# Two-layer hybrid decoder on one core: the last two expert pairs of each expert layer summed in one PSUM bank, in chunks of 512, 256 and 256 columns

## The chip, the cores and the metric

One Trainium2 chip, one of its cores. The time is device microseconds (us) from the start to the end of one execution; three executions of the kernel before gave a median of 892.34 us. Engines: PE is TensorE (matmuls; PEld its weight loads), DVE is VectorE, ACT is ScalarE, POOL is GpSimd, SP is SyncE, which here only starts transfers (DMAs). SBUF is the on-chip memory that the engines read, PSUM the banks that PE writes.

## The reference, cut to what matters

The kernel computes two decoder layers on 256 tokens of 1024 channels: an mLSTM mixer, then an attention mixer, and after each a grouped mixture of experts (16 experts, 2 per token, one shared router) and a layer norm. Only the end of the expert part is touched:

```python
def expert_block(args):
    xb, e = args
    return (jax.nn.silu(xb @ w_gate[e]) * (xb @ w_up[e])) @ w_down[e]

ys = lax.map(expert_block, (xs, block_expert)).reshape(cap, D)
y = jnp.zeros((T, D), h.dtype).at[buf_tok].add(ys * buf_w[:, None].astype(ys.dtype))
...
x = layer_norm(DEEPNORM_ALPHA * x + gate[:, None, :] * y, ln_g[layer, 1], ln_b[layer, 1])
```

So each token's output is the sum over its experts of (weight times expert output), times a gate row, added to alpha times the residual, and then normed over the 1024 channels.

## The kernel before, in words

**Tiling.** Tokens lie in two tiles of 128 partitions (`t` = 0, 1); `xt` holds 2 x 1024 channels. Experts go in pairs `b` = 0 to 7, 64 slots for each expert of a pair, so a pair fills 128 partitions. For each pair PE computes `pg` (gate) and `pu` (up), DVE multiplies them to `a`, PE transposes `a` to `aT`, and `down` computes `py` = `aT` times the down weights, a chunk of columns at a time, in bank `bankA`. `outputs` scales a chunk by the slot weights `wsl`, and `combine` multiplies it by the one-hot matrix `ohT[b]`, which brings slots back to tokens: `po`, one bank (`bankB`) for each token tile. Then DVE adds `po` to `acc`, which is `xt`.

**Two forms of the sum.** For pairs 0 to 6 `outputs` splits the scaled chunk into an upper part `yh` (rounded by ACT) and the rest `yl` (by DVE), and PE multiplies both by `ohT` in a fast format and sums them in the bank; `add_gated` (lines 544 to 548) then takes two DVE operations: `lntmpe` = `po` times gate, and `xt` += `lntmpe`. For the last pair (7) the gate is multiplied in before: `yg` = `py` times slot weight times gate (line 1239), a plain fp32 product with `ohT` (two passes on PE), and one DVE addition (line 1226). Pairs 0 to 6 have two chunks of 512 columns, pair 7 four of 256 (`LAST`, line 55).

**Layer norm.** `ln_stats` (line 550) takes `bn_stats` over four pieces of 256 columns for each token tile, `bn_aggr`, a square root on ACT and a reciprocal on DVE. In layer 0 `normalise` (line 566) then scales a whole token tile of 1024 columns, and the next stage transposes `xt` (`tk`, line 511) for the attention's keys. In layer 1 two DVE operations per half tile (lines 1388, 1389) and a store end the kernel.

**What sets the order.** `T` is PE's handle with `T.pinned`: while it is true, PE's instructions stay in program order. In `moe` that is so for nearly all of PE's work. The other engines are ordered by a scheduler by priority, except where `issue_after` puts an instruction behind another. `split` casts a weight tile to its upper part on ACT and takes the rest on DVE, with the priority `AHEAD` = 100. `T.pinned` and the like name no engine code lines of their own: every instruction that goes through a pinned handle is shown at line 135.

**Transfers.** All weights come through SP's one queue in pieces of 512 KB (`pieces`, line 224), each into a slot of a ring of buffers that the piece before has to have left. `ws[b, 2, i]` are the down weights of chunk `i`: a chunk of 512 columns is four pieces (two halves of the rows for each of two experts), a chunk of 256 columns two pieces (one for each expert, all rows).

**The overflow branch.** `rest` is a conditional block that is not taken here; each engine loads a register and branches (lines 1343, 1344). In layer 1 it stands between pair 7's `pu` and the last `down_part`.

## Time and profile before

| what | value |
|---|---|
| median of 3 executions | 892.34 us (891.92 to 893.64) |
| the profiled execution | 893.36 us |
| its span, first to last instruction | 891.7 us |
| PE busy | 854.3 us, 96% |
| DVE busy | 528.1 us, 59% |
| ACT busy | 327.4 us, 37% |
| read from HBM | 316.53 MB, 356 GB/s over the span |
| mean granted TensorE clock | 0.983 |

The span is 1.7 us shorter than the profiled execution's own time, and that execution is 1.0 us over the median. PE is shown busy nearly all the time, but matmuls are pipelined and a PE that works through products while the next weights are on their way looks the same as one that sets the pace; so the stages have to be looked at one by one. The end of layer 0's expert part lies at about 492 to 527 us of the span, that of layer 1 at about 856 us to the end.

### The profile page before, as it was taken

What the parts mean: (1) busy time and instruction counts of PE and PEld (TensorE: products, weight loads), DVE (VectorE), ACT (ScalarE), POOL (GpSimd) and SP (SyncE); (2) the same over time, 40 slices, a digit from 0 to 9 for tenths busy, and PEclk for the clock granted to TensorE, in tenths of its full rate; (3) what the DMA queues carried; (4) which work ended last, traced back from release to release, by engine and by line L of the source; (5) the groups of instructions that cost most, each with busy time, mean ns of one, the idle gap of its engine ahead of it and who ended that gap; (6) DMA issues with size and microseconds to landing.
All of it is one profiled execution on the core that took longest, in us unless ns stands there. A gap on an engine that the chain in (4) does not pass through costs nothing.

```text
span 891.7 us, 13434 instructions
## 1 busy us (share of the span) xinstructions
PE 854.3 (96%) x5049; PEld 532.2 (60%) x5052; DVE 528.1 (59%) x964; ACT 327.4 (37%) x549; POOL 7.8 (1%) x21
## 2 busy tenths in 40 slices
PE   8999999999999799999999889999989999999994
PEld 4888997688787434343343379887763433434332
DVE  2469997688898613342322489999973423233317
ACT  3458666366555411011121046667551111211120
POOL 0020000000000000000000000000000000000000
PEclk9999999999999999999999989999979999999997
DMA  9999887699987899999999999977978999999993
GB/s 324 394 393 351 294 337 251 228 410 413 370 268 258 327 397 407 406 406 407 407 406 407 367 410 412 363 278 258 373 289 310 408 406 407 407 407 407 406 400 120
DMA packets 161921, 318.56 MB, mean 357 GB/s; under 512 B 10120, under 2 KB 28168, under 8 KB 161848
## 3 DMA queue, kind: packets, MB, share of 16 engines
q1 hardware_dynamic: 161704, 317.42, 94.4%
q8 instruction: 42, 0.69, 0.3%
q14 instruction: 31, 0.25, 0.1%
q10 hardware_dynamic: 144, 0.20, 0.1%
HBM read 316.53 MB, written 1.05 MB: 356 GB/s over the span
## 4 chain that ended last, share of the span: by engine, by line
PE 43%; DMA 7%; DVE 3%; ACT 2%; issue 1%; DVEq 0%; SPq 0%; ACTq 0%
PE py L135 9%; PE pg L135 8%; PE pu L135 8%; DMA w<-in_moe_w_up_dram 3%; PE po L135 3%; PE ga L135 3%; DMA w<-in_moe_w_down_dram 2%; DMA w<-in_moe_w_gate_dram 1%; PE bo L1482 1%; PE bk L274 1%; PE bk L275 1%; PE bk L276 1%; PE by L274 1%; PE by L276 1%; PE by L275 1%; PE bq L274 1%
## 5 line engine op out<-in xcount | busy, mean ns | idle before, releaser
L1243 DVE SCALAR_TENSOR_TENSOR yl<-py,wsl,yh 128x512 fp32r<-128x512 f32 x28 | 21.0, 750 | 171.2 <-ACT yh L1242 171.2
L135 PE MATMUL py<-w,aT 128*64 128x512 f32 (+1 forms) x576 | 117.9, 547 | 1.7 <-DMA w<-in_moe_w_down_dram 1.7
L135 PE MATMUL pu<-w,xe 128*64 128x512 f32 x512 | 118.7, 596 | 0.2 <-DMA w<-in_moe_w_up_dram 0.2
L135 PE MATMUL pg<-w,xe 128*64 128x512 f32 x512 | 116.1, 596 | 0.0
L362 DVE SCALAR_TENSOR_TENSOR adacc<-ada,pk,adacc 128x1024 f32<-128x1024 f32 x70 | 89.4, 1278 | 0.2
L135 PEld LDWEIGHTS py<-w,aT 128*64 128x64 f32 x576 | 41.7, 137 | 73.6 <-issue 59.3
L135 PEld LDWEIGHTS pu<-w,xe 128*64 128x64 f32 x512 | 36.0, 137 | 67.5 <-issue 61.3
L135 PEld LDWEIGHTS pg<-w,xe 128*64 128x64 f32 x512 | 34.8, 137 | 63.9 <-issue 58.9
L547 DVE TENSOR_TENSOR lntmpe<-po,gate 128x512 f32<-128x512 f32 x56 | 36.1, 684 | 41.4 <-PE po L135 41.4
L1209 ACT COPY aT<-aT 128x512 f32<-128x512 f32 x16 | 9.4, 585 | 139.4 <-PE aT L135 139.4
L1242 ACT ACTIVATE yh<-py,wsl 128x512 fp32r<-128x512 f32 x28 | 19.2, 687 | 84.3 <-PE py L135 84.3
L525 ACT ACTIVATE xe<-ga,coef 128x256 f32<-128x256 f32 x32 | 16.1, 561 | 72.3 <-PE ga L135 72.3
L274 PE MATMUL z<-hh,wz 128*128 128x256 f32 x128 | 36.4, 284 | 0.0
L548 DVE TENSOR_TENSOR xt<-xt,lntmpe 128x512 f32<-128x512 f32 x56 | 36.0, 682 | 0.0
L275 PE MATMUL z<-hl,wz 128*128 128x256 f32 x128 | 36.0, 281 | 0.0
L276 PE MATMUL z<-hh,wz 128*128 128x256 f32 x128 | 36.0, 281 | 0.0
L1202 DVE TENSOR_TENSOR a<-a,pu 128x512 f32<-128x512 f32 x16 | 11.0, 688 | 36.3 <-PE pu L135 20.3
L135 PE MATMUL ga<-onehot,xh 128*128 128x256 f32 x128 | 31.3, 321 | 0.0
L135 PE MATMUL xm<-hh,win 128*128 128x256 f32 x144 | 28.8, 289 | 0.7 <-ACT hh L135 0.7
L1197 ACT ACTIVATE a<-pg 128x512 f32<-128x512 f32 x16 | 9.6, 597 | 52.2 <-PE pg L135 52.2
L135 PEld LDWEIGHTS ga<-onehot,xh 128*128 128x128 f32 x128 | 24.8, 218 | 5.9 <-DVE xt L548 4.1
L135 PE MATMUL ga<-onehot,xl 128*128 128x256 f32 x128 | 27.6, 282 | 0.0
(386 smaller groups left out, 1886.5 us busy)
## 6 DMA issues: line engine op xcount, KB each, us to landing
w<-in_moe_w_gate_dram SPq DMA_DIRECT2D x128, 512.0 KB, 10.2
w<-in_moe_w_up_dram SPq DMA_DIRECT2D x128, 512.0 KB, 10.2
w<-in_moe_w_down_dram SPq DMA_DIRECT2D x128, 512.0 KB, 10.2
ada<-in_w_ada_dram SPq DMA_DIRECT2D x112, 512.0 KB, 9.2
win<-in_a_w_in_dram SPq DMA_DIRECT2D x16, 512.0 KB, 8.2
wz<-in_a_w_in_dram SPq DMA_DIRECT2D x16, 512.0 KB, 10.0
wout<-in_a_w_out_dram SPq DMA_DIRECT2D x16, 512.0 KB, 8.4
wv<-in_a_wv_dram SPq DMA_DIRECT2D x8, 512.0 KB, 5.4
```

Source lines behind the costliest of these rows:

```text
L135: return self.tc.keep_in_program_order(f(*a, **kw))
L274: T.matmul(ps, l[0], r[0], start=start, stop=False, skip_group_check=True)
L275: T.matmul(ps, l[0], r[1], start=False, stop=False, skip_group_check=True)
L276: T.matmul(ps, l[1], r[0], start=False, stop=stop, skip_group_check=True)
L362: V.scalar_tensor_tensor(acc, w, c, acc, op0=OP.mult, op1=OP.add)
L525: A.activation(dst, ps, AF.Identity, bias=sh[:, k:k + 1], scale=sc[:, k:k + 1])
L547: V.tensor_tensor(tmp, y, gate[:, c], op=OP.mult)
L548: V.tensor_tensor(dst[:, t, c], dst[:, t, c], tmp, op=OP.add)
L1197: A.activation(a, pg, AF.Silu)
L1202: V.tensor_tensor(a, a, pu, op=OP.mult)
L1242: A.activation(yh, py, AF.Copy, scale=wsl[:, b:b + 1])
L1243: V.scalar_tensor_tensor(yl, py, wsl[:, b:b + 1], yh.bitcast(F32), op0=OP.mult, op1=OP.subtract)
```

## The change

- `LAST` gives the last pair three chunks, of 512, 256 and 256 columns. Its output is split into an upper and a lower part like that of the other pairs, in a tile `yl` that takes the place of `yg`.
- `down_last` replaces the last call of `down_part`. It computes pair 6's two chunks and pair 7's first two chunks of `py` before any sum; pair 7's transposes come behind pair 6's first chunk. `add(h)` then sums, for both token tiles, pair 6's two parts and pair 7's two parts of chunk `h` in one bank, so that DVE adds both pairs with one `add_gated`.
- Behind each addition DVE takes the `bn_stats` of the columns just added; `bn_aggr` and the root follow with the last chunk.
- `V.pinned` is set for this part: DVE's instructions keep program order too.
- In layer 0 the norm goes by halves of 512 columns, both token tiles of the first half first. `k_part(0)`, the first work of the attention, is put behind the last norm operation on DVE and now also behind the last root on ACT, and the first three `split` calls take the priorities 100, 35 and 60 from `ahead`.
- In layer 1 the norm's operations are in program order, tile by tile.

```diff
--- before.py
+++ after.py
@@ -52,7 +52,7 @@
 FILL = 8, 4, 14
 LEAD = 1, 4
 PE_ORDER = 1, 0, 4, 3, 2
-LAST = (0, 256), (256, 256), (512, 256), (768, 256)
+LAST = (0, 512), (512, 256), (768, 256)
 PAST = 4
 AT = 2, 6
 BACC = dict(dynamic_dma_scratch_size=1024)
@@ -257,11 +257,13 @@
         return lambda k: v[k // 4][:, k % 4:k % 4 + 2, :]
 
 
+    ahead = deque()
+
     def split(pool, src, name, dst=None, low=None):
 
         if dst is None:
             dst = pool.tile([P, 2, 2, 512], F32R, tag="whl", name=name)
-        with tc.high_priority(AHEAD):
+        with tc.high_priority(ahead.popleft() if ahead else AHEAD):
             A.copy(dst[:, 0], src)
             (low or V).tensor_tensor(dst[:, 1], src, dst[:, 0].bitcast(F32), op=OP.subtract)
         return [(dst[:, 0, i, :], dst[:, 1, i, :]) for i in range(2)]
@@ -1221,29 +1223,22 @@
                 for t in range(NT):
                     po = bankB(f"po{layer}_{b}_{t}{h}")[:, 0:w]
                     oh = ohT[b][:, P * t:P * t + P]
-                    if b == last_b:
-                        T.matmul(po, oh.bitcast(F32), y, start=True, stop=True)
-                        V.tensor_tensor(acc[:, t, o:o + w], acc[:, t, o:o + w], po, op=OP.add)
-                    else:
-                        for i in range(2):
-                            T.matmul(po, oh, y[i], start=i == 0, stop=i == 1)
-                        add_gated(t, o, w, po, gate, f"e{layer}_{b}_", acc)
+                    for i in range(2):
+                        T.matmul(po, oh, y[i], start=i == 0, stop=i == 1)
+                    add_gated(t, o, w, po, gate, f"e{layer}_{b}_", acc)
 
             def outputs(b, h, py):
 
                 o, w = chunks(b)[h]
                 if b == last_b:
-                    if not yg:
-                        yg.append(pm.tile([P, D], F32, tag="xe", name=f"yg{layer}"))
-                    y = yg[0][:, o:o + w]
-                    V.scalar_tensor_tensor(y, py, wsl[:, b:b + 1], gate[:, o:o + w], op0=OP.mult, op1=OP.mult)
-                    return y
-                yh, yl = [pm.tile([P, w], F32R, tag=f"{n}{h % 2}", name=f"{n}{layer}_{b}_{h}") for n in ("yh", "yl")]
+                    yh, yl = [ylast[0][:, z, o:o + w] for z in range(2)]
+                else:
+                    yh, yl = [pm.tile([P, w], F32R, tag=f"{n}{h % 2}", name=f"{n}{layer}_{b}_{h}") for n in ("yh", "yl")]
                 A.activation(yh, py, AF.Copy, scale=wsl[:, b:b + 1])
                 V.scalar_tensor_tensor(yl, py, wsl[:, b:b + 1], yh.bitcast(F32), op0=OP.mult, op1=OP.subtract)
                 return yh, yl
 
-            yg = []
+            ylast = []
 
             held = []
 
@@ -1252,17 +1247,48 @@
                     combine(*h)
                 held.clear()
 
-            def down_part(*pairs, hold=False):
-
-                for b, aT in pairs:
-                    for h, (o, w) in enumerate(chunks(b)):
-                        py = bankA(f"py{layer}_{b}_{h}")[:, 0:w]
-                        down(b, h, py, aT)
-                        if not hold:
-                            combine_held()
-                        held.append((b, h, outputs(b, h, py)))
-                if not hold:
-                    combine_held()
+            def down_chunk(b, h, aT):
+                py = bankA(f"py{layer}_{b}_{h}")[:, 0:chunks(b)[h][1]]
+                down(b, h, py, aT)
+                return outputs(b, h, py)
+
+            def down_part(b, aT):
+
+                for h in range(len(chunks(b))):
+                    held.append((b, h, down_chunk(b, h, aT)))
+
+            def down_last(aT, a):
+
+                y = [down_chunk(last_b - 1, 0, aT)]
+                aT7 = transposed_a(last_b, a, "oh")
+                y.append(down_chunk(last_b - 1, 1, aT))
+                ylast.append(pm.tile([P, 2, D], F32R, tag="xe", name=f"yl{layer}"))
+
+                def add(h):
+                    o, w = chunks(last_b)[h]
+                    po = [bankB(f"po{layer}_{t}_{h}")[:, 0:w] for t in range(NT)]
+                    for z, (oh, vs) in enumerate(((ohT[last_b - 1], [v[:, o % 512:o % 512 + w] for v in y[o // 512]]), (ohT[last_b], y7[h]))):
+                        for t in range(NT):
+                            for i, v in enumerate(vs):
+                                T.matmul(po[t], oh[:, P * t:P * t + P], v, start=(z, i) == (0, 0), stop=(z, i) == (1, 1))
+                    for t, (st, mv, rs) in enumerate(sts):
+                        add_gated(t, o, w, po[t], gate, f"e{layer}_{last_b}_", acc)
+                        for i in range(o // 256, (o + w) // 256):
+                            V.bn_stats(st[:, i, :], xt[:, t, 256 * i:256 * i + 256])
+                        if o + w == D:
+                            V.bn_aggr(mv, st)
+                            roots.append(A.activation(rs, mv[:, 1:2], AF.Sqrt, bias=epsc))
+
+                y7, roots = [], []
+                sts = [[small.tile([P, n], F32, tag=tag, name=f"{tag}n{t}") for tag, n in (("lnst", 24), ("lnmv", 2), ("lnrs", 1))] for t in range(NT)]
+                for s in sts:
+                    s[0] = s[0].rearrange("p (i j) -> p i j", j=6)
+                for h in range(len(chunks(last_b))):
+                    y7.append(down_chunk(last_b, h, aT7))
+                    if h:
+                        add(h - 1)
+                add(h)
+                return [s[1:] for s in sts], roots[-1]
 
             def overflow():
 
@@ -1362,7 +1388,7 @@
                 pg = gate_up(b + 1, xe, 0, "pg", lambda: aT.append(transposed_a(b, a)))
                 a = gated(b + 1, pg)
                 if b + 1 < last_b:
-                    down_part((b, aT[0]), hold=True)
+                    down_part(b, aT[0])
                     if b == AT[layer]:
                         load(b, 2, PAST)
                         T.pinned = False
@@ -1378,19 +1404,25 @@
                 rest()
             T.pinned = True
             preload(AF.Sqrt)
-            down_part((b, aT[0]), (last_b, transposed_a(last_b, a, "oh")))
+            V.pinned = True
+            sts, root = down_last(aT[0], a)
             T.pinned = False
-            for t in range(NT):
-                st = ln_stats(acc, t, f"n{layer}")
-                if last:
-                    for h in range(2):
-                        c = slice(512 * h, 512 * h + 512)
-                        V.scalar_tensor_tensor(acc[:, t, c], acc[:, t, c], st[0], row[0][:, c], op0=OP.subtract, op1=OP.mult)
-                        V.scalar_tensor_tensor(acc[:, t, c], acc[:, t, c], st[1], row[1][:, c], op0=OP.mult, op1=OP.add)
-                        nc.sync.dma_start(out[P * t:P * t + P, c], acc[:, t, c])
-                else:
-                    end = normalise(acc, t, st)
-        return None if last else end
+            if not last:
+                for h in range(2):
+                    c = slice(512 * h, 512 * h + 512)
+                    for t, (mv, rs) in enumerate(sts):
+                        if h == 0:
+                            V.reciprocal(rs, rs)
+                        end = V.tensor_scalar(xt[:, t, c], xt[:, t, c], mv[:, 0:1], rs, op0=OP.subtract, op1=OP.mult)
+                V.pinned = False
+                return end, root
+            for t, (mv, rs) in enumerate(sts):
+                V.reciprocal(rs, rs)
+                for h in range(2):
+                    c = slice(512 * h, 512 * h + 512)
+                    V.scalar_tensor_tensor(acc[:, t, c], acc[:, t, c], mv[:, 0:1], row[0][:, c], op0=OP.subtract, op1=OP.mult)
+                    V.scalar_tensor_tensor(acc[:, t, c], acc[:, t, c], rs, row[1][:, c], op0=OP.mult, op1=OP.add)
+                    nc.sync.dma_start(out[P * t:P * t + P, c], acc[:, t, c])
 
     end = moe(0, yA, gate, False)
     ptx.close()
@@ -1484,7 +1516,8 @@
         A.copy(oh_[:, e, :], po[:, 0:S])
         V.tensor_tensor(ol_[:, e, :], po[:, 0:S], oh_[:, e, :].bitcast(F32), op=OP.subtract)
 
-    with tc.issue_after(end.ins):
+    ahead.extend((AHEAD, 35, 60))
+    with tc.issue_after(end[0].ins), tc.issue_after(end[1].ins):
         queue((8, 9, 10, 11), RATE[2], PAIRS[1])
         k_part(0)
     modulated(xt, affine_split(qh, ql, scq, shq, "affq"), "tq")
```

**PE, end of layer 1.** `po_6_00` is the bank of pair 6, token tile 0, chunk 0; `py_7_0` pair 7's first chunk. Before:

```order
L135 MATMUL py_6_1_8216<-w_6_21_11_7846,aT_6_7911 64x512
L135 MATMUL po_6_00_8225<-yh_6_0_8212,ohT_6_7674 128x512
L135 MATMUL po_6_00_8225<-yl_6_0_8213,ohT_6_7674 128x512
L135 MATMUL po_6_10_8231<-yh_6_0_8212,ohT_6_7674 128x512
L135 MATMUL po_6_10_8231<-yl_6_0_8213,ohT_6_7674 128x512
L135 MATMUL py_7_0_8241<-w_7_20_00_7955,aT_7_8201 64x256
```

After, where `po_0_0` and `po_1_0` are the common banks of token tiles 0 and 1 for chunk 0:

```order
L135 MATMUL py_7_1_8242<-w_7_21_10_7960,aT_7_8209 64x256
L135 MATMUL po_0_0_8253<-yh_6_0_8200,ohT_6_7669 128x512
L135 MATMUL po_0_0_8253<-yl_6_0_8201,ohT_6_7669 128x512
L135 MATMUL po_1_0_8254<-yh_6_0_8200,ohT_6_7669 128x512
L135 MATMUL po_1_0_8254<-yl_6_0_8201,ohT_6_7669 128x512
L135 MATMUL po_0_0_8253<-yl_8224,ohT_7_7879 128x512 x2
L135 MATMUL po_1_0_8254<-yl_8224,ohT_7_7879 128x512 x2
L135 MATMUL py_7_2_8273<-w_7_22_00_7962,aT_7_8209 64x256
```

Pair 6's products with `ohT` stood right behind `py_6_1` and ahead of all of pair 7; now they stand behind the eight rows of `py_7_0` and the eight of `py_7_1`.

**DVE, end of layer 1.** Before, from pair 6's first addition to pair 7's second chunk:

```order
L547 TENSOR_TENSOR lntmpe_6_00_8228<-po_6_00_8225,gate_6590 128x512
L547 TENSOR_TENSOR lntmpe_6_10_8234<-po_6_10_8231,gate_6590 128x512
L548 TENSOR_TENSOR xt<-xt,lntmpe_6_00_8228 128x512
L548 TENSOR_TENSOR xt<-xt,lntmpe_6_10_8234 128x512
L1243 SCALAR_TENSOR_TENSOR yl_6_1_8238<-py_6_1_8216,wsl_6669,yh_6_1_8237 128x512
L1239 SCALAR_TENSOR_TENSOR yg_8262<-py_7_0_8241,wsl_6669,gate_6590 128x256
L547 TENSOR_TENSOR lntmpe_6_0512_8253<-po_6_01_8250,gate_6590 128x512
L547 TENSOR_TENSOR lntmpe_6_1512_8259<-po_6_11_8256,gate_6590 128x512
L548 TENSOR_TENSOR xt<-xt,lntmpe_6_0512_8253 128x512
L548 TENSOR_TENSOR xt<-xt,lntmpe_6_1512_8259 128x512
L1239 SCALAR_TENSOR_TENSOR yg_8262<-py_7_1_8264,wsl_6669,gate_6590 128x256
```

After, from the row that ends the work on pair 7's second chunk:

```order
L135 SCALAR_TENSOR_TENSOR yl_8224<-py_7_1_8242,wsl_6664,yl_8224 128x256
L135 TENSOR_TENSOR lntmpe_7_00_8263<-po_0_0_8253,gate_6585 128x512
L135 TENSOR_TENSOR xt<-xt,lntmpe_7_00_8263 128x512
L135 BN_STATS lnstn_8225<-xt 128x6 x2
L135 TENSOR_TENSOR lntmpe_7_10_8268<-po_1_0_8254,gate_6585 128x512
L135 TENSOR_TENSOR xt<-xt,lntmpe_7_10_8268 128x512
L135 BN_STATS lnstn_8228<-xt 128x6 x2
L135 SCALAR_TENSOR_TENSOR yl_8224<-py_7_2_8273,wsl_6664,yl_8224 128x256
L135 TENSOR_TENSOR lntmpe_7_0512_8294<-po_0_1_8284,gate_6585 128x256
L135 TENSOR_TENSOR xt<-xt,lntmpe_7_0512_8294 128x256
L135 BN_STATS lnstn_8225<-xt 128x6
L135 TENSOR_TENSOR lntmpe_7_1512_8298<-po_1_1_8285,gate_6585 128x256
```

Pair 6's eight operations are gone, and each operation on a chunk now reads what the operation just ahead of it wrote (`lntmpe`, then `xt`, then the statistics), where two token tiles alternated before; pair 7's third `yl` stands behind all of chunk 0.

**ACT, end of layer 0.** `lnrsn` is the root, `bk` the casts of the keys' first weights. Before:

```order
L1242 ACTIVATE yh_6_1_4877<-py_6_1_4856,wsl_3323 128x512
L265 CAST bk_0_5102<-wk_0_00_5092 128x1024
L265 CAST bk_2_5129<-wk_0_01_5094 128x1024
L541 ACTIVATE lnrsn_4960<-lnmvn_4959,epsc 128x1
L541 ACTIVATE lnrsn_4971<-lnmvn_4970,epsc 128x1
L265 CAST bk_4_5163<-wk_1_00_5096 128x1024
```

After:

```order
L1237 ACTIVATE yh_6_1_4865<-py_6_1_4856,wsl_3323 128x512
L1237 ACTIVATE yl_4869<-py_7_0_4876,wsl_3323 128x512
L1237 ACTIVATE yl_4869<-py_7_1_4887,wsl_3323 128x256
L1237 ACTIVATE yl_4869<-py_7_2_4918,wsl_3323 128x256
L1280 ACTIVATE lnrsn_4872<-lnmvn_4871,epsc 128x1
L1280 ACTIVATE lnrsn_4875<-lnmvn_4874,epsc 128x1
L267 CAST bk_0_5097<-wk_0_00_5087 128x1024
L267 CAST bk_2_5124<-wk_0_01_5089 128x1024
```

The casts stood ahead of the roots, and now stand behind them and behind three more scalings of pair 7.

## Rows read from the trace of the kernel before

**Rows 1.** Chain that ended last, 820 to 892: start us, length us, what.

```profile
823.05 6.87 PE py L135 x32
...
833.24 10.22 DMA w<-in_moe_w_gate_dram
...
853.82 10.23 DMA w<-in_moe_w_down_dram
...
864.09 1.93 PE py L135 x6
```

**Rows 2.** The same chain, 485 to 545 us.

```profile
501.92 1.93 PE py L135 x6
...
521.73 3.75 PE tk L511 x16
```

**Rows 3.** Single issues of pair 7's sixth piece: ns, start us; then us until landing.

```profile
L224 SPq DMA_DIRECT2D w<-in_moe_w_down_dram x1: 1269/1269/1269, 864.4 to 864.4; - x1
...
DMA to landing us min/median/max: 7.9/7.9/7.9
...
L224 SPq DMA_DIRECT2D w<-in_moe_w_down_dram x1: 1888/1888/1888, 502.2 to 502.2; - x1
...
DMA to landing us min/median/max: 8.5/8.5/8.5
```

**Rows 4.** Timeline of PE, layer 1's end: start us, length us, engine, line, operation, out<-in.

```profile
865.95 0.50 PE L135 MATMUL po<-yh,ohT 128*128 128x512 f32 x1
866.29 0.39 PE L135 MATMUL po<-yl,ohT 128*128 128x512 f32 x1
866.52 0.40 PE L135 MATMUL po<-yh,ohT 128*128 128x512 f32 x1
...
867.07 1.95 PE L135 MATMUL py<-w,aT 128*64 128x256 f32 x16
```

**Rows 5.** DVE's groups, 864 to 892: count | busy us, mean ns | idle before.

```profile
L1226 DVE TENSOR_TENSOR xt<-xt,po 128x256 f32<-128x256 f32 x8 | 3.3, 418 | 0.4
L556 DVE BATCH_NORM_STATS2 lnstn<-xt 128x6 f32<-128x256 f32 x8 | 3.0, 409 | 0.0
...
L1389 DVE SCALAR_TENSOR_TENSOR xt<-xt,lnrsn,lnrow 128x512 f32<-128x512 f32 x4 | 2.8, 742 | 0.0
...
L1239 DVE SCALAR_TENSOR_TENSOR yg<-py,wsl,gate 128x256 f32<-128x256 f32 x4 | 1.9, 480 | 1.6 <-PE py L135 1.6
```

**Rows 6.** Timeline of DVE, layer 1's end, neighbours that don't read each other.

```profile
870.46 1.29 DVE L547 TENSOR_TENSOR lntmpe<-po,gate 128x512 f32<-128x512 f32 x2 [0.20 <-PE po L135]
871.66 1.28 DVE L548 TENSOR_TENSOR xt<-xt,lntmpe 128x512 f32<-128x512 f32 x2
...
886.48 1.40 DVE L1389 SCALAR_TENSOR_TENSOR xt<-xt,lnrsn,lnrow 128x512 f32<-128x512 f32 x2
```

**Rows 7.** Timeline of DVE elsewhere, neighbours of which the second reads the first.

```profile
108.06 2.60 DVE L362 SCALAR_TENSOR_TENSOR adacc<-ada,pk,adacc 128x1024 f32<-128x1024 f32 x2
...
279.80 0.69 DVE L547 TENSOR_TENSOR lntmpm<-y,gate 128x512 f32<-128x512 f32 x1 [0.79 <-PE y L276]
280.52 0.69 DVE L548 TENSOR_TENSOR xt<-xt,lntmpm 128x512 f32<-128x512 f32 x1
```

**Rows 8.** Timelines of DVE and ACT where layer 0 ends.

```profile
520.13 0.26 DVE L557 BATCH_NORM_AGGREGATE lnmvn<-lnstn 128x2 f32<-128x24 f32 x1
...
521.78 0.81 DVE L566 TENSOR_SCALAR xt<-xt,lnmvn,lnrsn 128x1024 f32<-128x1024 f32 x1
...
518.44 1.99 ACT L265 CAST bk<-wk 128x1024 fp32r<-128x1024 f32 x2 [13.80 <-PE po L135]
...
523.59 1.02 ACT L525 ACTIVATE affk<-tk,coef 128x256 f32<-128x256 f32 x2 [1.84 <-PE tk L511]
```

**Rows 9.** Busy us of each engine in a stretch, granted clock, DMA share, GB/s.

```profile
519.00:527.00 8.00, 5.27 (x25) 5.05 (x26) 7.63 (x15) 4.37 (x9) 0.00 (x0) 0.61 1.04 411
```

**Rows 10.** SP's waits, 660 to 680: us in total, times, longest.

```profile
SPq L224 <- PE pg L135: 17.7, 6, 14.8
```

## The prediction

> **What bounds it now.** I read the chain of waits first, for the two places that the change touches. At layer 1's end the chain is DMA from 833.24 to 864.05: sixteen pieces of 512 KB in the 20.58 us between the rows at 833.24 and 853.82, 1.29 us each, and PE starts `py_6_1`'s last part when pair 6's last piece is there, at 864.09 [rows 1]. From there the reader should see a handover: PE takes 1.93 us, then PE, and from 879 on DVE alone, whose last operation ends at 886.48 + 1.40 = 887.88 [rows 6]. The rest of the span, 3.8 us, is the store and the close, which the change leaves alone. At layer 0's end the same step starts at 501.92, and PE's next stage, the transposes `tk`, at 521.73 [rows 2]. So each end is weights, then PE, then DVE. What counts is when DVE gets its first sum, and how long it works from then on.
>
> **The change, at layer 1's end.** PE's order is fixed, so the first sum (`po_0_0`, `po_1_0`) can't start before `py_7_1` is done, and that needs pair 7's sixth piece in the new order too (four for the chunk of 512, two for the first of 256). Before, that piece landed at 864.4 + 7.9 = 872.3 [rows 3]. From 864.05 that is 8.25 us for six, 1.37 each; the first four now have rows of 512 columns like those at 1.29 [rows 1], which gives 4 x 0.08 = 0.3 back: 872.0. The sixteen products of a chunk of 256 take 1.95: 873.95. The first bank is full after six of the eight products; neighbours start 0.23 to 0.34 apart and the last takes 0.40 [rows 4], so 0.34 + 4 x 0.23 + 0.40 = 1.65, less the 0.07 by which `po` starts ahead of `py`'s end (865.95 against 866.02): 875.5, and DVE starts at 875.6.
>
> Now DVE's work from there. Independent neighbours start before the former has ended: two multiplications of 512 columns take 1.29 though one takes 0.69, so a step is 0.60 [rows 6, 7]. With the same 0.08 overlap a 256-column operation is a step of 0.34 (418 ns), a `bn_stats` 0.33 (409), a scaling `yl` 0.40 (480), a norm operation 0.66 (742) [rows 5]. But where an operation reads what the one just ahead wrote, it waits for its end: the addition starts 0.72 after the multiplication, not 0.60, and two `adacc` take 2.60, twice 1.28 and a gap [rows 7]. That is 0.12 more for each such pair, and the new order makes them so. Chunk 0, for each tile: 0.60, 0.72, 0.45, 0.33 = 2.10, both 4.2. Then `yl` of the third chunk, 0.4. Four times a 256-column chunk: 0.34 + 0.46 + 0.45 = 1.25, together 5.0. Two `bn_aggr` of 0.26 [rows 8], step 0.17 + 0.12: 0.6. In all 10.2: 885.8. The roots lie on ACT beside that. The last part: eight norm operations 5.3, four of them reading the one ahead 0.5, two reciprocals 0.1, in all 5.9, plus the last one's 0.08: 891.8. Against 887.88 that is **3.9 us later**.
>
> What the change removes is real: eight operations of 512 columns (4.8), four `yg` (1.6) and eight additions of 256 (2.7), 9.1 us of DVE, against 6.6 added (`yl` 1.5, four operations of 512 2.4, eight of 256 2.7). PE loses the two-pass products as well. But before, DVE did 4.8 of its work in the time in which PE waited for or worked on pair 7; now it is empty until 875.6, so the saving falls where DVE idles and the remainder falls behind the last weights.
>
> PE's new waits for pieces of pair 7 queue pair 6's sums behind them; DVE waits for that. ACT's scalings and the early `yl` are done long before 875.6. `py_6_0` ahead of the branch costs nothing while `py_6_1`'s last piece comes at 864.05; without that cover it would be up to one chunk, 3.4 us (half of the 6.87 in [rows 1]).
>
> **At layer 0's end.** The sixth piece landed at 502.2 + 8.5 = 510.7 [rows 3]; less 0.3, 510.4. Plus 1.95, 1.58 and a step to DVE: 514.0. Plus 10.2: the last `bn_aggr` is out at 524.25, against 520.13 + 0.26 = 520.39 [rows 8]. Here the halves help: `tk` can start after a reciprocal and one half, not one whole tile of 0.81 [rows 8], and the root isn't behind a cast. A half I take at 0.43, half of 0.81 with some fixed part (bounds 0.40 and 0.81); with 0.2 for the reciprocal, `tk` starts at 524.85 instead of 521.73: 3.1 later. From there PE runs the same sixteen `tk`, four `tq` and two `bk` products before the first that needs the lower half `kl`, at the same low clock. The casts, 1.99 for two [rows 8], now stand between roots and `affk`: ACT is free for `affk` at about 526.6, 3 us after 523.59, so ACT is no later than PE, and DVE's `bk` rests end at 528.3, before PE wants `kl` at 529.6. The moved priorities change nothing else that PE waits for. I take **3.1 us**, bounds 2.2 (pieces at 1.29 from 501.87 on, the sixth at 509.6) and 4.3 (bank full at the same time, casts in series with `tk`).
>
> Does this reach the end? SP's queue stood 14.8 us waiting for layer 1's gate products to free buffers [rows 10], so the stream of layer 1's weights starts when that compute starts, and moves with it. I count it in full.
>
> Sum: 3.9 + 3.1 = 7.0 us. On the profiled execution 893.36 gives 900.4; the median lies 1.0 lower, so **899.3 us**, 0.8% slower. A difference within 0.2% (1.8 us) couldn't be told from no change.
>
> **Rivals.** (a) No gap between operations that read each other. For it: most DVE neighbours in the trace overlap by 0.08. Against: [rows 7], the very same pair of operations. Eighteen gaps at layer 1's end, fourteen at layer 0's, 32 x 0.12 = 3.8 less: 895.5. The Trainium skill, VectorE: DVE Perf Modes, section "The DRAIN you can't avoid", holds that the next operation waits for the pipe to empty whether or not a semaphore stands between, so that only the number of operations counts; by that rule this case would hold. The trace disagrees: 0.60 and 0.72 for one kind of operation.
>
> (b) Layer 0's delay is swallowed on the way, because transfers run on while PE is late. For it: DMA is busy through 519 to 527 [rows 9]. Against: [rows 10], the stream has to wait for buffers later on. Then only 3.9 stays: 896.2.
>
> (c) Not slower: the last pair's weights are there before PE asks, and PE runs through both chunks without a wait. Then layer 1's first sum comes at 866.02 + 3.44 + 1.95 + 1.6 = 873.0, 2.6 sooner than I took, and layer 0's at 503.85 + 7.0 = 510.85, 3.15 sooner; 7.0 - 5.75 = 1.25 stays: 893.6, no change that can be told. It decides from the point where the sixth piece lands within 5.4 us of pair 6's last. For it: before, PE waited for no piece of pair 7. Against: six pieces at 1.29 are 7.7 us, and the same queue brings them.
>
> (d) The clock. In 519 to 527 the mean granted clock was 0.61, of levels 2.4 and 1.2 GHz, after PE's last sum at 518.4, where ACT's cast was released [rows 8, 9]. Now PE has a longer hole there, about 519 to 525. If the low level lasts 3.5 us further into the `bk` products, half of that is lost, 1.7: 901.0.
>
> **How the numbers follow.** Forecast 0.70, (a) 0.07, (b) 0.08, (c) 0.07, (d) 0.08. The forecast's own bounds: layer 0 by -0.9 and +1.2, layer 1 by half a us for the pieces, so 897.8 to 901. The range takes in (a), (b) and (d) and the half us about them: 895.0 to 901.7; below lies (c), with some of (a). Faster 0.03 from (c) with shorter gaps, same 0.07, slower 0.90.
>
> **What would show it.** In the changed kernel's trace: DVE idle until about 11.5 us after the step that starts at 864.09 in [rows 1], then the first multiplication, and no idle time to the end; additions 0.03 us after the multiplication's end; PE waiting for down weights inside `py_7_0` and `py_7_1`; `tk` about 23 us after `py_6_1`'s last part starts in layer 0, where it was 19.8; the last store about 4 us later against the same step. If DVE's first sum stands at 9 us after that step, (c) holds; if DVE's steps overlap, (a); if layer 1's `py_6_1` is not about 3 us later, (b).

## The result, and the profile after

| | median of the runs, us | lowest to highest | profiled execution, its span |
|---|---|---|---|
| before | 892.75 | 891.92 to 893.64 | 893.36, 891.7 |
| changed | 900.87 | 900.29 to 902.76 | 900.58, 898.5 |

The ratio is 1.0094, with a 95% interval of 1.0079 to 1.0109: the change costs 0.9%, some 8 us. The forecast was 899.3 within 895.0 to 901.7, slower by 7.0.

**Layer 1's end.** The first view is SP's issues of two pieces of down weights in the changed kernel: ns of the issue and its start in us, then the us until the piece has landed. The first is the last piece of pair 6, the second the sixth of pair 7.

```profile
L224 SPq DMA_DIRECT2D w<-in_moe_w_down_dram x1: 880/880/880, 856.0 to 856.0; - x1
...
DMA to landing us min/median/max: 10.2/10.2/10.2
...
L224 SPq DMA_DIRECT2D w<-in_moe_w_down_dram x1: 1897/1897/1897, 863.7 to 863.7; - x1
...
DMA to landing us min/median/max: 10.4/10.4/10.4
```

So pair 6's last piece is there at 866.2 and pair 7's sixth at 874.1, 7.9 us later, where the prediction had 8.0. Next the timeline of VectorE from there on (start us, length us, engine, line, operation, out<-in, tile, type, count, and in brackets the idle time before it and what ended that):

```profile
878.59 0.69 DVE L135 TENSOR_TENSOR lntmpe<-po,gate 128x512 f32<-128x512 f32 x1 [0.58 <-PE po L135]
879.32 0.69 DVE L135 TENSOR_TENSOR xt<-xt,lntmpe 128x512 f32<-128x512 f32 x1
...
888.56 0.26 DVE L135 BATCH_NORM_AGGREGATE lnmvn<-lnstn 128x2 f32<-128x24 f32 x1
888.74 0.11 DVE L135 RECIPROCAL lnrsn<-lnrsn 128x1 f32<-128x1 f32 x1
888.76 0.73 DVE L135 SCALAR_TENSOR_TENSOR xt<-xt,lnmvn,lnrow 128x512 f32<-128x512 f32 x1
...
893.94 0.75 DVE L135 SCALAR_TENSOR_TENSOR xt<-xt,lnrsn,lnrow 128x512 f32<-128x512 f32 x1
```

From the first sum at 878.59 nothing but VectorE is late: its next operation starts where the last one ends. The addition at 879.32 starts 0.73 after the multiplication and not 0.60 as the neighbours in [rows 6] do, since it reads what that wrote, as in [rows 7]. The last `bn_aggr` ends at 888.56 + 0.26 = 888.82, 10.23 us after the first sum (predicted 10.2), the last norm operation at 894.69, 5.9 us after the reciprocal's start (predicted 5.9). From pair 6's last landing to that end it is 28.5 us; before, from the landing at 864.05 in [rows 1] to 887.88 [rows 6], 23.8.

One interval is longer than predicted. The first sum comes 878.59 - 866.2 = 12.4 us after pair 6's last piece, where 11.5 was forecast. TensorE's timeline at the same place shows why:

```profile
861.11 1.93 PE L135 MATMUL py<-w,aT 128*64 128x512 f32 x6 [0.19 <-DMA w<-in_moe_w_down_dram]
865.87 0.66 PE L135 MATMUL aT<-cs,a 128*128 128x128 f32 x4 [2.83 <-ACTq L1370]
866.46 10.51 PE L135 MATMUL py<-w,aT 128*64 128x512 f32 x48
876.90 0.50 PE L135 MATMUL po<-yh,ohT 128*128 128x512 f32 x1
```

Behind `py_6_0` TensorE stands 2.83 us for ACT's sequencer at line 1370, the branch to the overflow block. ACT comes to that branch late because two things now stand ahead of it, the scaling `yh_6_0` and the four copies into `lnrow`. In the kernel before, the copies ran early, while TensorE worked on pair 7's `pu`, and the scaling came behind the branch. Here is the row of the copies in the kernel before, then ACT's two rows in the changed one, where the copies are queued behind a scaling that has to wait for `py_6_0`:

```profile
847.32 2.06 ACT L495 ACTIVATE lnrow<-lnps 128x512 f32<-128x512 f32 x4
```

```profile
863.14 0.69 ACT L1237 ACTIVATE yh<-py,wsl 128x512 fp32r<-128x512 f32 x1 [13.63 <-PEq L1370]
863.72 2.05 ACT L497 ACTIVATE lnrow<-lnps 128x512 f32<-128x512 f32 x4
```

And after the hole TensorE runs at the low level. This is the view of stretches (busy us and count of PE, PEld, DVE, ACT, POOL, then the granted clock, DMA's share and GB/s):

```profile
863.00:866.00 3.00, 0.17 (x2) 0.13 (x2) 0.75 (x1) 2.63 (x5) 0.00 (x0) 1.00 1.05 404
866.00:870.40 4.40, 4.40 (x16) 1.51 (x18) 0.00 (x0) 0.58 (x1) 0.00 (x0) 0.61 1.05 402
870.40:877.00 6.60, 6.60 (x41) 2.64 (x37) 1.50 (x2) 1.37 (x2) 0.00 (x0) 1.00 0.82 292
```

From 866.46 on 48 products run without a wait for weights. Had TensorE been at full clock, `py_7_1` would have waited for its sixth piece and ended at 874.1 + 1.95 = 876.05; it ended at 866.46 + 10.51 = 876.97, 0.9 later.

**Layer 0's end.** The same handover, first VectorE's timeline, then TensorE's with its next stage:

```profile
514.71 0.69 DVE L135 TENSOR_TENSOR lntmpe<-po,gate 128x512 f32<-128x512 f32 x1 [0.61 <-PE po L135]
...
524.68 0.26 DVE L135 BATCH_NORM_AGGREGATE lnmvn<-lnstn 128x2 f32<-128x24 f32 x1
524.86 0.10 DVE L135 RECIPROCAL lnrsn<-lnrsn 128x1 f32<-128x1 f32 x1
525.00 0.55 DVE L135 TENSOR_SCALAR xt<-xt,lnmvn,lnrsn 128x512 f32<-128x512 f32 x1
```

```profile
502.67 5.52 PE L135 MATMUL py<-w,aT 128*64 128x512 f32 x16 [0.17 <-DMA w<-in_moe_w_down_dram]
...
525.60 3.71 PE L513 MATMUL tk<-cs,xt 128*128 128x128 f32 x16 [5.52 <-DVE xt L135]
```

Here the step that waits for pair 6's last piece is at 502.67, 0.75 later than in [rows 2]; that lies ahead of the changed place. From it to `tk` it is 22.93 us, against 521.73 - 501.92 = 19.81 in [rows 2]: 3.1 longer, as predicted. The sums and statistics take 10.23 again.

The account of the two profiled executions: 0.75 from before layer 0's end, 3.1 at it, 4.65 at layer 1's end (28.5 against 23.84), and 1.7 less on the way between the two ends, in all 6.8, which is the difference of the spans. What that 1.7 is worth is weighed in the experiments. A further 0.4 us lies outside the spans: the time is 2.1 us over the span in each of the four executions of the changed kernel, and 1.7 in those of the kernel before. `aT7_first`, `early_sum` and `after_warm` have 2.0 to 2.1 too, all other kernels 1.7; why is open.

### The profile page after: what moved, and what is told of

Its sections match the earlier page's. It is cut to its first block, busy times and chain, and to the rows that moved or that the text cites. A ratio compares the mean times of both kernels' runs of the same rounds, so it can differ in the third digit from the quotient of the medians.

```text
span 898.5 us, 13365 instructions
## 1 busy us (share of the span) xinstructions
PE 852.2 (95%) x5017; PEld 527.8 (59%) x5020; DVE 524.9 (58%) x956; ACT 330.7 (37%) x555; POOL 7.8 (1%) x21
## 5 line engine op out<-in xcount | busy, mean ns | idle before, releaser
L135 PE MATMUL py<-w,aT 128*64 128x512 f32 (+1 forms) x544 | 122.3, 577 | 2.8 <-DMA w<-in_moe_w_down_dram 2.6
L1238 DVE SCALAR_TENSOR_TENSOR yl<-py,wsl,yh 128x512 fp32r<-128x512 f32 x24 | 18.0, 751 | 160.8 <-ACT yh L1237 160.8
L549 DVE TENSOR_TENSOR lntmpe<-po,gate 128x512 f32<-128x512 f32 x48 | 30.9, 684 | 30.8 <-PE po L135 30.8
L550 DVE TENSOR_TENSOR xt<-xt,lntmpe 128x512 f32<-128x512 f32 x48 | 30.9, 682 | 0.0
L135 PE MATMUL po<-yl,ohT 128*128 128x512 f32 (+1 forms) x84 | 26.8, 365 | 1.4 <-DVE yl L135 1.4
## 6 DMA issues: line engine op xcount, KB each, us to landing
w<-in_moe_w_gate_dram SPq DMA_DIRECT2D x128, 512.0 KB, 10.2
w<-in_moe_w_up_dram SPq DMA_DIRECT2D x128, 512.0 KB, 10.2
w<-in_moe_w_down_dram SPq DMA_DIRECT2D x128, 512.0 KB, 10.2
```

The lines of the kernel that those rows point to most:

```text
L135: return self.tc.keep_in_program_order(f(*a, **kw))
L549: V.tensor_tensor(tmp, y, gate[:, c], op=OP.mult)
L550: V.tensor_tensor(dst[:, t, c], dst[:, t, c], tmp, op=OP.add)
L1238: V.scalar_tensor_tensor(yl, py, wsl[:, b:b + 1], yh.bitcast(F32), op0=OP.mult, op1=OP.subtract)
```

## The experiments

`b_halves`, `halves_warm`, `b_chunks` and `best` are made from the kernel before, the others from the changed one. Every time has its own runs of the kernel before beside it, and the ratios are to those.

### One layer at a time

In `l0_only` layer 1 keeps the end of the kernel before, chunks, sums, statistics and norm, in `l1_only` layer 0 does, with its casts where they stood before (there the condition is `layer != 1`).

```
+            if layer != 0:
+                down_old((b, aT[0]), (last_b, transposed_a(last_b, a, "oh")))
...
             sts, root = down_last(aT[0], a)
```

> The new end in layer 0 alone; layer 1 ends as before, with its four chunks of 256. Theory (late first sum in each layer, layer 0's part arriving in full): 3.1 us over the kernel before, 895.9. Rival (layer 0's delay swallowed on the way to layer 1): no difference, 892.8. In the trace of the changed kernel pair 6's last piece of layer 1 landed only 2.2 us later, so 894.9 would mean that about two thirds arrive.

> The new end in layer 1 alone. Theory: the predicted 3.9 us, and up to 0.9 us more, because TensorE stands 2.83 us at the overflow branch that now comes behind py_6_0: 896.7 to 897.6. If layer 0's delay is swallowed (rival), this one must carry nearly all of the 8.1 us: 900.9.

Measured: `l0_only` 895.2, ratio 1.0019 (1.0008 to 1.0030), 1.7 us slower; `l1_only` 897.39, ratio 1.0041 (1.0026 to 1.0056), 3.7 us slower. Layer 1's term of 3.9 holds in this kernel, which has no low clock behind the branch (below). Layer 0's delay arrives at the end, so it is not swallowed whole; whether all of the 3.1 arrives, or of the 2.6 that this kernel's own trace shows, this run alone can't say, for its interval reaches from 0.7 to 2.7.

`l1_only` has the same hole at the branch as the changed kernel, but not the same end of it. Three views of it: TensorE's timeline, the stretch behind the hole with its granted clock, and VectorE's first sum:

```profile
864.47 0.66 PE L136 MATMUL aT<-cs,a 128*128 128x128 f32 x4 [2.83 <-ACTq L1391]
865.06 7.51 PE L136 MATMUL py<-w,aT 128*64 128x512 f32 x34
872.73 1.94 PE L136 MATMUL py<-w,aT 128*64 128x256 f32 x14 [0.16 <-DMA w<-in_moe_w_down_dram]
```

```profile
864.50:869.50 5.00, 5.00 (x26) 1.98 (x28) 0.00 (x0) 1.27 (x2) 0.00 (x0) 1.00 1.06 401
```

```profile
876.29 0.69 DVE L136 TENSOR_TENSOR lntmpe<-po,gate 128x512 f32<-128x512 f32 x1 [0.60 <-PE po L136]
```

Here the clock stayed at 1.00, `py_7_1` did wait for its pieces, and the first sum comes 11.5 us after pair 6's last landing (864.8), as predicted. So the wait at the branch is covered by the weights, and what isn't covered is the low level when it follows. The two kernels differ in layer 0 too, but their instructions here are the same.

### Without the hole at the branch

`aT7_first` writes the four transposes of pair 7 ahead of `py_6_0`. They need the last `a`, so in layer 1 the branch comes ahead of `py_6_0` again.

```
-                y = [down_chunk(last_b - 1, 0, aT)]
                 aT7 = transposed_a(last_b, a, "oh")
+                y = [down_chunk(last_b - 1, 0, aT)]
```

> The changed kernel with pair 7's transposes written ahead of py_6_0, so that the branch comes ahead of py_6_0 again, as in the kernel before. Theory that the branch wait costs: py_7_1 then ends on its weights, 874.08 + 1.95 = 876.0 instead of 876.97, and the time falls by 0.9 us, 900.0. Rival (py_7_1 is bound by its weights anyway and the wait is hidden, as the prediction put it): no difference, 900.9.

Measured: 899.35, ratio 1.0066 (1.0047 to 1.0085), 5.9 us over the kernel before. In TensorE's timeline the wait of 2.83 is gone, and `py_7_1` waits for its piece:

```profile
859.33 0.63 PE L135 MATMUL aT<-cs,a 128*128 128x128 f32 x4 [1.00 <-DVEq L1370]
859.88 6.62 PE L135 MATMUL py<-w,aT 128*64 128x512 f32 x26
...
874.59 1.94 PE L135 MATMUL py<-w,aT 128*64 128x256 f32 x14 [0.70 <-DMA w<-in_moe_w_down_dram]
```

Its first sum comes 11.5 us after pair 6's last landing instead of 12.4, and the whole end of layer 1 takes 27.6 us instead of 28.5: the expected 0.9. The times agree with that, but their intervals overlap (1.0047 to 1.0085 against 1.0079 to 1.0109), so the 0.9 is shown by the trace and not by the time.

### The gaps between operations that read each other

`alternate` does each step of a chunk for both token tiles before the next step. Operations and products are the same.

```
-                    for t, (st, mv, rs) in enumerate(sts):
-                        add_gated(t, o, w, po[t], gate, f"e{layer}_{last_b}_", acc)
...
+                    for t in range(NT):
+                        V.tensor_tensor(tmp[t], po[t], gate[:, c], op=OP.mult)
+                    for t in range(NT):
+                        V.tensor_tensor(acc[:, t, c], acc[:, t, c], tmp[t], op=OP.add)
+                    for i in range(o // 256, (o + w) // 256):
+                        for t in range(NT):
+                            V.bn_stats(sts[t][0][:, i, :], xt[:, t, 256 * i:256 * i + 256])
```

> The changed kernel with the two token tiles alternating on VectorE, so that no operation of a chunk reads what the one just ahead of it wrote; same operations, same products. Theory (0.12 us for each of 14 direct dependencies in a layer): from the first sum to the last bn_aggr 8.5 us instead of 10.2, 1.7 us a layer, 897.5 for the whole. Rival (a) of the prediction, that such gaps don't exist and only the number of operations counts: no difference, 900.9.

Measured: 897.05, ratio 1.0043 (1.0027 to 1.0059), 3.8 us over the kernel before, some 4.5 less than the changed kernel. VectorE's timeline at layer 1's end:

```profile
878.23 1.29 DVE L135 TENSOR_TENSOR lntmpe<-po,gate 128x512 f32<-128x512 f32 x2 [0.58 <-PE po L135]
879.43 1.28 DVE L135 TENSOR_TENSOR xt<-xt,lntmpe 128x512 f32<-128x512 f32 x2
880.63 1.40 DVE L135 BATCH_NORM_STATS2 lnstn<-xt 128x6 f32<-128x256 f32 x4
...
886.31 0.38 DVE L135 BATCH_NORM_AGGREGATE lnmvn<-lnstn 128x2 f32<-128x24 f32 x2
```

From the first sum to the end of the last `bn_aggr` it is 886.69 - 878.23 = 8.46 us, where 8.5 was expected and the changed kernel has 10.23. The same operations take 1.77 us less once none reads what the one just ahead wrote, 0.126 for each of the 14 places. Rival (a) of the prediction falls. The Trainium skill, VectorE: DVE Perf Modes, section "The DRAIN you can't avoid", has the next operation wait until the pipe is empty, and adds that one which is not held starts earlier. By the first rule alone, which is what the prediction took from it, the order would have made no difference, and here the measurement decides.

### An earlier first sum

`early_sum` puts pair 6's share of chunk 0 into the bank ahead of `py_7_0` and closes the bank right behind it. VectorE's operations are those of the changed kernel, with the scaling `yl` of the second chunk between the two token tiles.

```
+                p0 = sums(0)
+                y7.append(down_chunk(last_b, 0, aT7))
+                close(0, p0)
+                add(0, p0, (0,))
+                y7.append(down_chunk(last_b, 1, aT7))
+                add(0, p0, (1,))
```

> The changed kernel with chunk 0 summed at once: pair 6's share goes into the bank ahead of py_7_0, pair 7's right behind py_7_0, so the first sum needs four pieces of pair 7 instead of six; VectorE's work is the same. Theory (the loss is the late first sum): the first sum comes 2.5 to 3 us earlier in each layer, from pair 6's last landing to the last operation of VectorE in layer 1 about 25.5 us instead of 28.5, the time 5 us below the changed kernel's, about 896. Rival (VectorE's own work is the bound, and new waits between the chunks give the lead back): at most 1 us less, 900.

Measured: 900.26, ratio 1.0086 (1.0069 to 1.0104): within its interval the changed kernel's time. The rival is nearer. VectorE's rows:

```profile
874.72 0.75 DVE L135 SCALAR_TENSOR_TENSOR yl<-py,wsl,yl 128x512 fp32r<-128x512 f32 x1 [3.90 <-ACT yl L1237]
876.06 0.69 DVE L135 TENSOR_TENSOR lntmpe<-po,gate 128x512 f32<-128x512 f32 x1 [0.59 <-PE po L135]
...
878.93 0.48 DVE L135 SCALAR_TENSOR_TENSOR yl<-py,wsl,yl 128x256 fp32r<-128x256 f32 x1 [0.66 <-ACT yl L1237]
```

The first sum is 10.7 us behind pair 6's last landing instead of 12.4. But with the sum right behind its products, ACT's scaling, VectorE's `yl` and the last products stand in a row between `py_7_0` and the sum, and `py_7_1` behind those; VectorE then waits 0.66 us for the second chunk, and its stretch to the last `bn_aggr` grows from 10.2 to 11.4. Of 1.7 us of lead 1.2 goes back. But the clock stayed at 1.00 behind the hole in this profile (865 to 870), so 0.9 of the lead in layer 1 is the clock's: against `l1_only` and `aT7_first`, at the same clock, the lead is 0.8 and the whole end 0.4 longer. Layer 0, where both kernels had 1.00 up to the sums, is the cleaner comparison: the first sum comes 2.6 us sooner (9.5 behind pair 6's last landing, not 12.1), the stretch is the same 1.2 longer, and `tk` comes 1.4 sooner. My theory that only the late first sum counts was too simple: the lag of one chunk in the changed kernel has a use, it hides this handover.

### Without the common bank

`apart` sums pair 6 on its own ahead of `py_7_0` and leaves only pair 7's share for the sums behind.

```
+                own(0)
+                own(1)
                 for h in range(len(chunks(last_b))):
                     y7.append(down_chunk(last_b, h, aT7))
```

> The changed kernel without the common bank: pair 6's share is summed on its own ahead of py_7_0 (eight more operations of 512 columns on VectorE in each layer, and the same count of products less one wait), the rest as in the changed kernel. Theory (what lies behind the last weights counts, and the common bank takes nothing away there): VectorE does the extra 4.8 us in the time in which it stood idle, TensorE has four products less between py_7_1 and the first sum, and the time falls by 0.9 us a layer, to about 899. Rival (VectorE's amount of work counts): 4.8 us a layer more, 910.

Measured: 900.83, ratio 1.0097 (1.0078 to 1.0117), the same as the changed kernel, with eight more operations of 512 columns on VectorE in each layer. So VectorE's amount of work isn't what counts (the rival asked for 910), and the common bank, which saves those operations, gains nothing. The forecast 0.9 a layer isn't in the time either. In layer 0 the first sum does come 1.2 us sooner (10.9 us behind pair 6's last landing, not 12.1); in layer 1 it doesn't. Rows of TensorE and ACT there, then VectorE's:

```profile
872.68 5.38 PE L135 MATMUL py<-w,aT 128*64 128x512 f32 x32
...
876.38 0.69 ACT L1237 ACTIVATE yl<-py,wsl 128x512 fp32r<-128x512 f32 x1 [5.43 <-PE py L135]
```

```profile
871.65 0.68 DVE L135 TENSOR_TENSOR lntmpe<-po_s,gate 128x512 f32<-128x512 f32 x1
...
876.34 0.69 DVE L135 TENSOR_TENSOR xt<-xt,lntmpe 128x512 f32<-128x512 f32 x1
877.10 0.75 DVE L135 SCALAR_TENSOR_TENSOR yl<-py,wsl,yl 128x512 fp32r<-128x512 f32 x1
878.61 0.48 DVE L135 SCALAR_TENSOR_TENSOR yl<-py,wsl,yl 128x256 fp32r<-128x256 f32 x1 [0.76 <-ACT yl L1237]
879.01 0.68 DVE L135 TENSOR_TENSOR lntmpe<-po,gate 128x512 f32<-128x512 f32 x1
```

VectorE's extra work fills 871.65 to 877.03, and ACT is done with its part of pair 7's first chunk at 876.38 + 0.69 = 877.07, so the scaling at 877.10 is not held up: VectorE's hole was just large enough. What is late is TensorE. It has pair 6's eight products ahead of `py_7_0` now, behind the same 2.83 us at the branch, and then runs pair 7's 32 products without a wait for weights until 872.68 + 5.38 = 878.06, though the sixth piece was there at 874.2. So the products that were taken out from behind `py_7_1` stand ahead of it, and in layer 1 the wait at the branch comes on top: `py_7_1` ends 11.8 us behind pair 6's last landing there, and 9.9 us in layer 0.

### All three together

`combo` is `early_sum`, `alternate` and `aT7_first` in one, and in layer 1's norm the two operations of a half no longer stand next to each other.

> early_sum, alternate and aT7_first together, and in layer 1's norm the two operations of one half no longer next to each other. Theory: 0.9 for the branch, 2.5 a layer for the first sum, 1.7 a layer for the gaps and 0.2 in the norm add up to 9.5 us below the changed kernel's, 891.4, a little below the kernel before. If the waits between the chunks become the bound (the third chunk's weights land last), 895.

Measured: 895.24, ratio 1.0030 (1.0019 to 1.0042), 2.7 us over the kernel before: the best form of the changed end, and still not the end of before. The second of the two expected cases came: the first sum is 9.2 us behind pair 6's last landing, but VectorE then waits for the third chunk, and its stretch to the last `bn_aggr` is 10.2 us again:

```profile
881.15 0.48 DVE L135 SCALAR_TENSOR_TENSOR yl<-py,wsl,yl 128x256 fp32r<-128x256 f32 x1 [1.21 <-ACT yl L1237]
```

### TensorE's clock in layer 0's hole

`after_warm` and `halves_warm` add products that nobody reads behind the last sums of layer 0, six to the changed kernel and three to `b_halves` (below).

```
             sts, root = down_last(aT[0], a)
+            if not last:
+                stay_warm(6, f"n{layer}")
```

> The changed kernel with six products on TensorE that nobody reads, written behind layer 0's last sums, so that TensorE's hole of 5.5 us ahead of tk is filled. Theory (layer 0's delay is partly paid by the clock: the granted clock was 0.53 in 522 to 525 and 0.50 in 525 to 528, and TensorE worked at the low level from 525.6 to about 529): without the low level 1.7 us less, 899.2. Rival (something else is late then, as kl is in l1_only, where no low level came and TensorE waited 1.17 us for kl): 0 to 0.5 us less, 900.6.

> b_halves with three such products in its hole of 2.65 us behind layer 0's last sums. Theory of the clock: its mean granted clock in 520 to 540 was 0.91, so 3.6 us at the low level and 1.8 us lost: 1.5 us below b_halves, ratio to the kernel before 0.997. Rival (late operands take the place of the clock): no difference to b_halves, 0.9987.

Measured: `after_warm` 899.9, ratio 1.0079 (1.0065 to 1.0094); `halves_warm` 892.57, ratio 0.9990 (0.9980 to 1.0000). No difference to their kernels, but the experiment didn't do what it should. TensorE's timeline of `after_warm`, and two stretches of it:

```profile
518.88 1.48 PE L135 MATMUL warmn<-onesq 128*128 128x512 bf16 x5
524.57 0.44 PE L513 MATMUL tk<-cs,xt 128*128 128x128 f32 x2 [4.20 <-DVE xt L135]
```

```profile
522.00:525.00 3.00, 0.43 (x2) 0.20 (x2) 2.79 (x10) 1.35 (x3) 0.00 (x0) 1.00 1.05 414
525.00:528.00 3.00, 2.78 (x14) 2.78 (x14) 3.00 (x5) 2.96 (x7) 0.00 (x0) 0.50 1.03 421
```

The products are of bf16 and took 1.48 us in all (five of the six have a row), so 4.2 us of the hole were left, and the low level came 3 us later than without them, just as `tk` began.

What a filled hole would bring can still be read, because two of the other profiles happen to have no low level behind this hole, `l1_only` (layer 0 as before) and `best` (the norm by halves). The second row is `b_halves`, whose low level lasts 3.4 us into the work:

```profile
521.00:529.00 8.00, 6.70 (x51) 5.93 (x52) 7.94 (x16) 6.69 (x12) 0.00 (x0) 1.00 1.04 412
```

```profile
520.49:524.00 3.51, 3.31 (x16) 3.05 (x17) 3.47 (x6) 3.46 (x7) 0.00 (x0) 0.54 1.05 410
```

From the start of `tk` to the end of the last `bk` product it is 28.54 us in `best` and 28.65 in `b_halves`; with the whole tile's norm it is 29.01 in `l1_only`, 29.02 in `b_chunks` with 3.4 us at the low level, and 29.57 in the kernel before with 5.9. So 3.4 us at the low level cost some 0.1 at most, because other operands are late then (in `l1_only` TensorE waits 1.17 us for `kl`): the rival of both expectations is borne out. A longer low level does cost: in `alternate` and `early_sum` it lasts 6.0 us, and the way is 29.7 us where the changed kernel, with 3.4, has 28.53.

### The parts that the kernel before can take

`b_halves` is the kernel before with layer 0's norm by halves, written ahead of the loop that holds the old norm, and the casts behind the roots; `b_chunks` is the kernel before with the chunks of 512, 256, 256; `best` has both. None has the common bank.

```
+            if not last:
...
+                for h in range(2):
+                    c = slice(512 * h, 512 * h + 512)
+                    for t, (mv, rs) in enumerate(sts):
+                        if h == 0:
+                            V.reciprocal(rs, rs)
+                        end = V.tensor_scalar(xt[:, t, c], xt[:, t, c], mv[:, 0:1], rs, op0=OP.subtract, op1=OP.mult)
...
-LAST = (0, 256), (256, 256), (512, 256), (768, 256)
+LAST = (0, 512), (512, 256), (768, 256)
```

> The kernel before with one part of the change alone: layer 0's norm by halves and the weight casts behind the roots. Theory (the halves help, the casts cost nothing): from the last bn_aggr to the first tk 0.66 us as in the changed kernel instead of 1.34, so 0.7 us less, 892.1. Rival (the casts that now come behind the roots hold up the bk products and eat it): 892.8 or more.

> The kernel before with one part of the change alone, the chunks of the last pair: 512, 256, 256 instead of four of 256. TensorE has the same columns, VectorE two scalings and two additions less per layer, about 1 us of work. Theory (in the kernel before the end is TensorE's chain of py and po behind pair 6, and VectorE waits 0.8 us for each chunk): one such handover less per layer, up to 0.8 us a layer, 891.5 to 892.8. Rival (the chunk of 512 makes VectorE's first product of pair 7 wait for four pieces, and that is late): 1 us a layer more, 894.5.

> The two parts of the change that the traces call gains, on the kernel before and without the common bank: the chunks of 512, 256, 256 of b_chunks and the norm by halves with the casts behind the roots of b_halves. In their traces b_chunks is 0.57 us shorter from pair 6's last landing to the last norm operation of layer 1 and 0.5 us from pair 6's last landing to tk in layer 0, b_halves 0.68 us in the latter. Theory (the parts add): 1.75 us below the kernel before, ratio 0.998. Rival (both shorten the same wait): b_halves' 0.9987 or no difference.

Measured: `b_halves` 891.86, ratio 0.9987 (0.9975 to 0.9999); `b_chunks` 892.85, ratio 0.9995 (0.9983 to 1.0007), a difference that can't be told; `best` 891.4, ratio 0.9989 (0.9978 to 0.9999). The halves do gain what the step on them said. The timelines of VectorE and of TensorE in `b_halves`:

```profile
519.57 0.26 DVE L1392 BATCH_NORM_AGGREGATE lnmvn<-lnstn 128x2 f32<-128x24 f32 x1
...
519.89 0.55 DVE L135 TENSOR_SCALAR xt<-xt,lnmvn,lnrsn 128x512 f32<-128x512 f32 x1
```

```profile
520.49 0.45 PE L513 MATMUL tk<-cs,xt 128*128 128x128 f32 x2 [2.65 <-DVE xt L135]
```

From the end of the last `bn_aggr` (519.83) to `tk` it is 0.66 us, where it was 521.73 - 520.39 = 1.34 [rows 2, 8]. `best` and `b_halves` are the two kernels whose whole interval lies below the kernel before, by about 1 us and only just (both intervals end at 0.9999); that the chunks add to it isn't shown.

### Does a delay of layer 0 reach the end?

The thirteen kernels that were timed answer this better than the one run. For each the table has, against the kernel before, how much longer the way from pair 6's last landing to `tk` is in layer 0, how much longer the way from there to the last norm operation is in layer 1 (both from its profile, 19.86 and 23.84 before), their sum, and what the times gave (ratio less 1, by 893).

| kernel | layer 0 | layer 1 | sum | measured |
|---|---|---|---|---|
| changed | 3.1 | 4.6 | 7.7 | 8.4 |
| l0_only | 2.6 | 0.0 | 2.6 | 1.7 |
| l1_only | 0.0 | 3.75 | 3.75 | 3.7 |
| aT7_first | 3.1 | 3.8 | 6.9 | 5.9 |
| alternate | 1.3 | 3.2 | 4.5 | 3.8 |
| early_sum | 1.7 | 4.2 | 5.9 | 7.7 |
| apart | 1.9 | 5.0 | 6.9 | 8.7 |
| combo | 0.75 | 1.3 | 2.0 | 2.7 |
| after_warm | 2.9 | 4.7 | 7.6 | 7.1 |
| b_halves | -0.7 | 0.0 | -0.7 | -1.2 |
| halves_warm | -0.7 | 0.0 | -0.7 | -0.9 |
| b_chunks | -0.5 | -0.6 | -1.1 | -0.4 |
| best | -1.15 | -0.6 | -1.7 | -1.0 |

Measured less sum is 0.2 on the mean and between -1.0 and 1.8, and the intervals of the measured ones are 0.9 to 1.7 us to either side. A rival that swallows layer 0's part would need the layer 1 column alone to do as well; it is 1.7 short in `l0_only`, 3.8 in the changed kernel and 3.5 in `early_sum`. So layer 0's delay reaches the end. That all of it does is shown less sharply: with one factor for each column, the measured times fit best with 0.7 of layer 0's column and 1.2 of layer 1's, each known to some 0.2. The 1.7 us less between the two ends in the changed kernel's profile belong to that execution: from `tk` to layer 1's first gate product it is 145.3 to 147.6 us in the fourteen profiles, 147.6 in that of the kernel before and 145.75 in that of the changed one, but 147.0 in `l1_only`, which has layer 0 as before, and 147.6 in `alternate`, which has the changed end there. 1.0 of the 1.8 between the kernel before and the changed one lies in the stretch from `tk` to the last `bk` product and goes with the length of the low level, as shown above.

## Why the prediction was right

The direction and the size came out as forecast, by the mechanism that was named: the first sum behind the last pair's sixth piece, and behind it a VectorE that is the bound.

- **The sixth piece** was put 8.0 and 8.5 us behind pair 6's last; it was 7.9, and 511.1 - 502.6 = 8.5 in layer 0. That closes rival (c), which needed 5.4.
- **The first sum** was put 11.5 us behind pair 6's last landing. It is 11.5 in `l1_only` and `aT7_first` and 12.1 in layer 0, as predicted there. In the changed kernel's layer 1 it is 12.4. The step that failed is the sentence that `py_6_0` ahead of the branch costs nothing under the cover of `py_6_1`'s last piece. The cover was there for the wait of 2.83 us itself; what it didn't hide was the low clock that follows such a hole, 0.9 us. The prediction looked at what the branch moves on TensorE, and not at what then stands ahead of the branch on ACT. Its sign "PE waiting for down weights inside `py_7_0` and `py_7_1`" came in layer 0 (0.65 us at 511.12) and in `l1_only`, but not in the changed kernel's layer 1, where TensorE was late itself.
- **VectorE's chain** of 10.2 us was 10.23 in both layers, and its 0.12 for a dependent neighbour was 0.126 in `alternate`. Layer 1's norm was 5.9, as worked out.
- **The halves**: 0.66 from the last `bn_aggr` to `tk`, predicted 0.6. The half was put at 0.43; it lasts 0.55, and the reciprocal behind it starts 0.46 after it does. Layer 0's sum of 3.1 held.
- **That layer 0's part reaches the end** held, by the table; rival (b) falls. "In full" is within the noise of the times, and not shown more closely than that.
- **Rival (d)**, a low level that lasts further into the `bk` products, didn't come in this profile. Its 3.5 us were an assumption from no row. The granted clock of the changed kernel was 0.53 in 522 to 525, 0.50 in 525 to 528, 0.83 in 528 to 531 and 1.00 from there. With `tk` at 525.6 that is some 3.4 us of work at the low level; before it was 0.50 and 0.56 in 522 to 525 and 525 to 528 with `tk` at 521.73, some 5.9 us. The hole is longer, but more of the low level falls into it. That is not fixed by the kernel: with the changed end in layer 0, `early_sum` worked 6.0 us at the low level, about as long as the kernel before.
- **The sum** of 7.0 lacks the 0.9 at the branch and the 0.4 outside the span. How many of the timed executions have the 0.9 isn't known, since only one was profiled. The profiled execution took 900.58 where 900.4 was worked out, but with 1.7 us saved between the two ends and 0.75 lost ahead of them, which are of that execution. The median, 900.87, is 1.6 over the forecast. That 900.58 and 900.4 lie so close together is in part luck. The range's upper end of 901.7 is 0.2 above what rival (d) and its half us give; nothing hangs on it.

## What to carry to other kernels

An operation saved on an engine was worth something here only behind the point where that engine's last input arrives: VectorE is busy 3.2 us less in the changed kernel (524.9 us against 528.1), and the time rose, since the work saved had stood in its idle time and what is left moved behind the last weights; `apart`, with eight more such operations in each layer, took the same time. Where such a tail is left, let independent tiles alternate, so that no operation reads what the one ahead has just written: 0.126 us for each such place. When an instruction is let past a branch, look at every engine that has to reach the branch, not only at the one that gains.
